# One hybrid encoder block on one core: a PSUM pool of its own for the conv taps' running sum, the relative-bias table made near the front, and the conv weights' transposes moved behind the first projection

## The chip, the cores and the metric

The kernel runs on one core of one Trainium2 chip. Its time is the device time of one execution in microseconds (us). Five engines work side by side, each through its own list of instructions in order: TensorE does matmuls (PE in the profile; PEld is its weight load), VectorE (DVE) and ScalarE (ACT) do elementwise work and read what matmuls leave in PSUM, GpSimd (POOL) does elementwise work in SBUF, and SyncE (SP) issues the DMA transfers. They meet through semaphores alone. PSUM, into which every matmul writes, is used here as eight banks of 512 float32 words for each of 128 partitions.

## The reference

One layer with 1024 tokens of width 1024, all in float32. Cut to what matters:

```python
h = rms_norm(x, norm_in_g)
proj = h @ w_in                       # split into q, k, v, z_a, q_idx, k_idx, w_idx, glu_in, z_b, gate_a, gate_b
# sparse attention: 8 index heads give scores; the 256 best keys of each query are kept
scores = einsum(relu(q_idx . k_idx), w_idx);  top_idx = top_k(scores, 256)
logits = q . k[top_idx] * 0.125 + rel_bias[t5_bucket(top_idx - q_pos)]
attn = softmax(logits) @ v[top_idx]
y_a = (attn * silu(z_a)) @ w_branch_a
u = glu_in[..., :512] * sigmoid(glu_in[..., 512:])
c = causal_depthwise_conv(u, conv_w) + conv_b          # 31 taps, 512 channels
y_b = (silu(layer_norm(c)) * silu(z_b)) @ w_branch_b
x = x + (sigmoid(gate_a) * y_a + sigmoid(gate_b) * y_b) @ w_out
x = x + sigmoid(rms_norm(x) @ w_ple_gate) * (p @ w_ple_proj)
out = rms_norm(x, final_norm_g)
```

The relative bias depends on the distance between key and query alone, so the kernel makes one table of 8 heads by 384 distances with a small matmul (`rel_bias` against a one-hot matrix), writes it to DRAM and spreads it over 128 partitions there.

## The kernel before

**Arithmetic.** Each float32 operand of a projection is split into a high part and the remainder (`w_hi`, `w_lo`, `h_h`, `h_l`), and a product is three matmuls: lines L199, L200 and L201 in `mm3`. A projection of 128 output rows by 512 tokens is 24 such matmuls into one PSUM bank. `mbank` hands the banks out in rotation from a list (`mbanks`), and ScalarE or VectorE empties a bank afterwards.

**Order in the program.** The front normalises and transposes `x` (L249 transposes, L254 and L255 the split). `glu(0)` makes the first 128 channels of `u`. Then come the index keys (72 rows), the index scores in three double banks called `wide` (L361 and L362, relu on ScalarE L366, weighted sum on VectorE L370), and `glu(1..3)`. Then VectorE runs the 31 taps of four channel groups (L299), while TensorE projects gates (`next_gate`: `z_a`, `z_b`, the branch gates; emptied by ScalarE L452). Between taps a binary search finds the 256th best score of each query: ScalarE counts signs (L419), VectorE narrows (L415, L424, L425, L437); the search ends in masks (L503 to L516, the last row L511). The four channel groups are normalised with two pairs of matmuls against a matrix of ones (L585 for the mean, L598 for the variance; `st` names the two banks they write). Then queries (L552 on ScalarE and L553 on VectorE empty their banks), keys (L564, L565) and values (L647, L648) are projected. Then attention, head by head: scores (L710, L711; the mask is added and the maximum taken by VectorE L718), transposes of probabilities (L770 to L778, emptied by L781 and L782), probabilities times values (L731), emptied by L736, L737 and L742; the projection of branch B is fed in between (L809 to L811). Branch A (L866), the output projection and the last gate end the program.

**Who sets the order.** The tile framework records the program, a scheduler orders each engine's list by priorities (`hp()` raises them) and by its own model of the machine, and inserts semaphore waits between instructions that touch the same tile. `tc.issue_after` pins an instruction behind another one. `stage()` hands out 512-word SBUF buffers in rotation.

**PSUM.** Banks 0 and 1 belong to the pool `ps` for the whole program. Banks 2 to 7 are `pi` in the front and `wide` during the index scores. After that a pool `pn` holds banks 2 to 5 and one tile `acc` of 1024 words, that is banks 6 and 7. The taps sum up in `acc`. When they are done, `acc` is used as two banks to the end of the program:

```python
psum += [pn.tile([128, 512], F32, name=f"bank{b}") for b in range(2, 6)]
acc[0] = pn.tile([128, 1024], F32, name="acc")
psum += [acc[0][:, 0:512], acc[0][:, 512:1024]]
```

From L616 on, `mbanks` runs over all eight banks, 6 and 7 one after the other. In attention the scores use banks 4, 5 and 6 (`LB`), the transposes 0 and 1 (`PTB`), the products with the values 2 and 7 (`OB`), and branch B bank 3.

**The two other places.** The 31 tap weights, the bias and the norm's weights arrive as 34 rows (`cv`, L267 to L270) and four transposes (L272, copied by L273 into `ccol`) turn them; the first use is `first_tap(0)` (L294). The relative-bias table is made at L535 to L542, after the gates: two loads, the matmul L539, the copy L540, the store into `d_tv` (L541) and its spreading into `d_tp` (L542), which `load_head` reads in attention.

Of the kernel before, what the change touches and what calls it, by code (L numbers as in the profile page):

```python
# [8 lines left out]
F32 = mybir.dt.float32  # L9
# [9 lines left out]
NH = 8  # L19
# [19 lines left out]
def hybrid_block(ctx: ExitStack, tc: tile.TileContext, x, p, norm_in_g, w_in, conv_w, conv_b,  # L39
                 conv_ln_g, conv_ln_b, w_branch_a, w_branch_b, w_out, ple_norm_g, w_ple_gate,  # L40
                 w_ple_proj, rel_bias, final_norm_g, onehot, out):
    nc = tc.nc
    def hp():
        return tc.high_priority(offset=8000)
# [23 lines left out]
    psum = [pp.tile([128, 512], F32, name=f"bank{b}") for b in range(2)]  # L68
    pn = tc.alloc_tile_pool(name="pi", bufs=1, space=bass.MemoryType.PSUM)
# [4 lines left out]
    def bank(b, n=512):  # L74
        if b < len(psum):
            return psum[b][:, 0:n]
        o = b % 2 * 512
        return wide[(b - 2) // 2][:, o:o + n]
# [15 lines left out]
    d_tv = dr.tile([NH, 384], F32, name="d_tv")  # L94
    d_tp = dr.tile([NH, 128, 384], F32, name="d_tp")
# [10 lines left out]
    def const(n):  # L106
        o = cw[0]
        cw[0] += n
        return cslab[:, o:o + n]

    ident = const(128)
# [4 lines left out]
    ccol = const(4 * 34).rearrange("p (c k) -> p c k", c=4)  # L116
# [33 lines left out]
    def stage(dt=F32):  # L150
        sn[0] += 1
        return spools[sn[0] % len(spools)]("g", dt)
# [7 lines left out]
    def load_w(src, cols, nk_=NK, g=None, pool=None, prio=True):  # L160
        if pool is None:
            wn[0] += 1
            pool = wpools[wn[0] % len(wpools)]
        w = sum(c[1] for c in cols)
        per = min(nk_, pool.tags["raw"][0] // w)
        his, los = [], []
        for a in range(0, nk_, per):
            raw = k3(pool("raw")[:, 0:per * w], per)
            hi = k3(pool("hi", F32R)[:, 0:per * w], per)
            lo = k3(pool("lo", F32R)[:, 0:per * w], per)  # L170
            o = 0
            for c0, n in cols:
                nc.sync.dma_start(raw[:, :, o:o + n], src[:, a:a + per, c0:c0 + n])
                o += n
            with hp() if prio else nullcontext():
                if g is None:
                    nc.scalar.copy(hi, raw)  # L177
                    nc.gpsimd.tensor_tensor(lo, raw, f(hi), op=OP.subtract)  # L178
                else:
                    for k in range(per):  # L180
                        gk = g[:, a + k:a + k + 1]
                        nc.scalar.activation(hi[:, k], raw[:, k], AF.Copy, scale=gk)
                        nc.vector.scalar_tensor_tensor(lo[:, k], raw[:, k], gk, f(hi[:, k]), OP.mult, OP.subtract)
            his += [hi[:, k] for k in range(per)]
            los += [lo[:, k] for k in range(per)]
        return his, los
# [16 lines left out]
    last_mm = [None]  # L203
# [3 lines left out]
    def mbank(n=512, m=128):  # L207
        b = mbanks[0][mmb[0] % len(mbanks[0])]
        mmb[0] += 1
        return bank(b, n)[0:m]  # L210

    def proj(w, c0, m, n0, n):
        o = mbank(n, m)
        mm3(o, cut(w, c0, m), hcut(n0, n))
        return o
# [14 lines left out]
    aux = bank(1)  # L230
# [10 lines left out]
    for t in range(8):  # L241
        nc.vector.tensor_scalar(xt[t], xt[t], rx[:, t:t + 1], None, OP.mult)
        if t % 4 == 3:
            c = slice((t - 3) % 4 * 128, (t % 4 + 1) * 128)
            for k in range(NK):
                b = k if t < 4 else 2 + k % 6
# [19 lines left out]
    cv = stage()  # L266
# [1 line left out]
    nc.sync.dma_start(cv[31:32], conv_b)  # L268
    nc.sync.dma_start(cv[32:33], conv_ln_g)
    nc.sync.dma_start(cv[33:34], conv_ln_b)  # L270
    for c in range(4):
        nc.tensor.transpose(aux[:, 34 * c:34 * (c + 1)], cv[0:34, 128 * c:128 * (c + 1)], ident[0:34, 0:34])  # L272
    nc.vector.tensor_copy(ccol, aux[:, 0:136].rearrange("p (c k) -> p c k", c=4))  # L273

    def glu(c, wg=None, wa=None):
        if wg is None:
            wg = load_w(win, [(C_GB + 128 * c, 128)])
            wa = load_w(win, [(C_GA + 128 * c, 128)])
        U[c] = UP("u")
        nc.gpsimd.memset(U[c][:, 0:30], 0.0)  # L280
        for hf in range(2):
            og = proj(wg, 0, 128, hf * 512, 512)
            s_ = stage()
            with hp():
                nc.scalar.activation(s_, og, AF.Sigmoid)
            oa = proj(wa, 0, 128, hf * 512, 512)
            with hp():
                nc.vector.tensor_tensor(U[c][:, 30 + hf * 512:30 + hf * 512 + 512], oa, s_, op=OP.mult)

    acc = [None]  # L290

    def first_tap(c):
        A[c] = UP("u", words=1024)
        nc.scalar.activation(A[c], U[c][:, 0:1024], AF.Identity, bias=ccol[:, c, 31:32], scale=ccol[:, c, 0:1])  # L294
# [5 lines left out]

    w_ki = load_w(win, [(C_KI, 72)])
    glu(0, w_g0, w_a0)
    first_tap(0)
    for j in range(1, EARLY + 1):
        tap(0, j)
# [28 lines left out]
    for m in range(4):  # L334
# [4 lines left out]
        for t0, n in ((256, 256), (512, 512)):  # L339
            o = proj(w, 0, 128, t0, n)  # L340
            c = slice(t0 - 256, t0 - 256 + n)
# [32 lines left out]
    pw.release()  # L374
    pn = tc.alloc_tile_pool(name="pn", bufs=1, space=bass.MemoryType.PSUM)
    psum += [pn.tile([128, 512], F32, name=f"bank{b}") for b in range(2, 6)]
    acc[0] = pn.tile([128, 1024], F32, name="acc")
    psum += [acc[0][:, 0:512], acc[0][:, 512:1024]]

    SY = Pool("sy", [("g", 512, 4)], side="right")  # L380
    spools[0:] = [SP, SY, SX, SP, SY]
# [131 lines left out]
    for ch in ENDS:  # L513
        c = slice(ch[0] - 2, ch[-1] - 1)
# [17 lines left out]
        next_gate()  # L532


    rb, oh, tv = stage(), stage(), stage()  # L535
    nc.sync.dma_start(rb[0:32, 0:8], rel_bias)
    nc.sync.dma_start(oh[0:32, 0:384], onehot)
    rbo = mbank(384)
    nc.tensor.matmul(rbo[0:8], rb[0:32, 0:8], oh[0:32, 0:384], start=True, stop=True)  # L539
    nc.vector.tensor_copy(tv[0:8, 0:384], rbo[0:8])  # L540
    nc.sync.dma_start(d_tv, tv[0:8, 0:384])  # L541
    nc.sync.dma_start(d_tp, d_tv.unsqueeze(1).to_broadcast([NH, 128, 384]))  # L542


    def queries(m):
        w = load_w(win, [(C_Q + 128 * m, 128)])
        for hf in range(2):
            t0 = hf * 512
            o = proj(w, 0, 128, t0, 512)
            a_, b_ = stage(F32R), stage(F32R)  # L550
            with hp():
                nc.scalar.activation(a_, o, AF.Copy, scale=0.125)  # L552
                nc.vector.scalar_tensor_tensor(b_, o, 0.125, f(a_), OP.mult, OP.subtract)  # L553
                for e in range(2):
                    nc.sync.dma_start(d_q[2 * m + e, 0, :, t0:t0 + 512], f(a_)[64 * e:64 * e + 64])
                    nc.sync.dma_start(d_q[2 * m + e, 1, :, t0:t0 + 512], f(b_)[64 * e:64 * e + 64])
# [10 lines left out]
                nc.sync.dma_start(d_kl[128 * m:128 * (m + 1), t0:t0 + 512], f(b_))  # L567


    st = [bank(6), bank(7)]  # L570
    z = [UP("u", words=1024) for s in range(2)]

# [401 lines left out]
    WQ.close()  # L974
    SP.close()
    CP.close()
    pn.release()
    pp.release()

# [46 lines left out]
```

## Time and profile before

| what | value |
| --- | --- |
| three runs of the kernel | 1068.12, 1069.9 and 1070.03 us, median 1069.9 us |
| the profiled execution | 1071.17 us, of which the span from the first to the last instruction is 1069.4 us |
| mean granted TensorE clock in it | 0.98 |
| instructions in the span | 13995 |

The profiled execution lies 1.3 us above the median of the runs. A row of the profile names the line of the code, the engine, the tiles as out<-in, and the time. In a list of waits the columns are the total in us, the number of waits and the longest one. In a timeline the columns are start and duration in us, and a bracket gives the idle time before the instruction and what ended it.

### The profile page before, as it was taken

How to read it: one execution, taken by the hardware profiler on the slowest of the kernel's cores; microseconds unless marked ns; L12 is line 12 of the kernel's file. 1: busy time of each engine (PE TensorE's matmuls, PEld its weight loads, DVE VectorE, ACT ScalarE, POOL GpSimd, SP SyncE). 2: the span in 40 equal slices, each digit the busy share in tenths (PEclk: the TensorE clock that was granted, in tenths of full speed). 3: DMA queues.
4: the chain of work that ended last, by engine and by line, in shares of the span. 5: the costliest groups of instructions: out<-in, count | busy, mean ns of one | idle time of the engine just before them, and what ended most of it. 6: DMA issues, size and time to landing. Idle time of an engine off the chain costs nothing.

```text
span 1069.4 us, 13995 instructions
## 1 busy us (share of the span) xinstructions
PE 1004.9 (94%) x4993; PEld 838.6 (78%) x4993; DVE 710.2 (66%) x1418; ACT 517.4 (48%) x976; POOL 282.8 (26%) x260
## 2 busy tenths in 40 slices
PE   7999999999999899994999988888799999999896
PEld 6778888888888688883889977777688778888785
DVE  5395545999999999997921177677674952242444
ACT  7444544566666788655311175555552412351422
POOL 5230202222231221352130043333423612100111
PEclk9999999999999899997999999999999999999999
DMA  7221110332232353234542375454227752020012
GB/s 246 64 60 40 40 40 21 89 116 81 89 109 80 126 162 108 60 108 97 122 149 86 97 190 145 133 153 124 89 77 262 253 215 75 5 79 1 21 59 98
DMA packets 95205, 111.45 MB, mean 104 GB/s; under 512 B 6341, under 2 KB 64765, under 8 KB 95135
## 3 DMA queue, kind: packets, MB, share of 16 engines
q1 hardware_dynamic: 95134, 110.56, 34.0%
q8 instruction: 39, 0.64, 0.2%
q14 instruction: 32, 0.25, 0.1%
HBM read 81.16 MB, written 30.95 MB: 105 GB/s over the span
## 4 chain that ended last, share of the span: by engine, by line
PE 72%; DVE 16%; ACT 4%; issue 4%; DMA 2%; POOL 1%; SPq 1%; DVEq 0%; POOLq 0%; ACTq 0%
PE bank L199 17%; PE bank L201 17%; PE bank L200 17%; DVE i_j L437 3%; PE acc L199 2%; PE acc L201 2%; PE acc L200 2%; PE acc L731 2%; DVE e_P L718 1%; PE bank L731 1%; PE bank L770 1%; PE wide L361 1%; PE wide L362 1%; DVE u_u L299 1%; DVE f_sa L869 1%
## 5 line engine op out<-in xcount | busy, mean ns | idle before, releaser
L199 PE MATMUL bank<-h_h,w_hi 128*128 128x512 f32 (+2 forms) x672 | 260.8, 389 | 1.5 <-DVE h_l L255 1.1
L201 PE MATMUL bank<-h_h,w_lo 128*128 128x512 f32 (+2 forms) x672 | 259.9, 387 | 0.0
L200 PE MATMUL bank<-h_l,w_hi 128*128 128x512 f32 (+2 forms) x672 | 259.8, 387 | 0.0
L178 POOL TENSOR_TENSOR w_lo<-w_raw,w_hi 128x1024 fp32r<-128x1024 f32 (+1 forms) x57 | 143.4, 2517 | 378.4 <-ACT w_hi L177 373.1
L419 ACT ACTIVATE i_aj<-i_S,c_d 128x384 bf16<-128x384 f32 (+3 forms) x150 | 124.4, 830 | 72.6 <-DVE c_d L415 62.3
L199 PEld LDWEIGHTS bank<-h_h,w_hi 128*128 128x128 f32 (+1 forms) x672 | 126.1, 188 | 29.7 <-issue 1.7
L200 PEld LDWEIGHTS bank<-h_l,w_hi 128*128 128x128 f32 (+1 forms) x672 | 126.3, 188 | 25.9 <-issue 0.5
L201 PEld LDWEIGHTS bank<-h_h,w_lo 128*128 128x128 f32 (+1 forms) x672 | 126.1, 188 | 26.0 <-issue 0.2
L299 DVE SCALAR_TENSOR_TENSOR acc<-u_u,c_c,acc 128x1024 f32<-128x1024 f32 x100 | 128.7, 1287 | 2.4
L177 ACT CAST w_hi<-w_raw 128x1024 fp32r<-128x1024 f32 (+1 forms) x57 | 59.2, 1039 | 82.0 <-PE acc L200 29.4
L199 PE MATMUL bank<-w_hi,g_h 128*128 128x512 f32 x224 | 87.3, 393 | 1.4 <-ACT s_g L955 1.4
L201 PE MATMUL bank<-w_hi,g_l 128*128 128x512 f32 x224 | 88.1, 395 | 0.1
L200 PE MATMUL bank<-w_lo,g_h 128*128 128x512 f32 x224 | 87.5, 391 | 0.0
L370 DVE SCALAR_TENSOR_TENSOR i_S<-wide,c_c,i_S 128x384 f32<-128x384 f32 (+5 forms) x42 | 39.2, 949 | 42.5 <-ACT wide L366 42.2
L701 POOL TENSOR_TENSOR e_mt<-m_m,ea_tp 128x256 f32<-128x256 bf16 (+1 forms) x64 | 40.7, 650 | 90.8 <-DVE c_c L718 80.0
L366 ACT ACTIVATE wide<-wide 128x384 f32<-128x384 f32 (+5 forms) x48 | 35.3, 741 | 46.8 <-PE wide L362 45.8
L721 ACT ACTIVATE e_P<-e_P,c_c 128x384 f32<-128x384 f32 (+4 forms) x64 | 49.3, 773 | 3.7 <-DVE c_c L718 3.1
L199 PEld LDWEIGHTS bank<-w_hi,g_h 128*128 128x128 f32 x224 | 42.1, 188 | 10.1 <-ACT s_g L955 1.8
L201 PEld LDWEIGHTS bank<-w_hi,g_l 128*128 128x128 f32 x224 | 42.1, 188 | 9.0 <-DVE g_l L871 0.5
L200 PEld LDWEIGHTS bank<-w_lo,g_h 128*128 128x128 f32 x224 | 42.1, 188 | 8.6
L781 ACT CAST e_pth<-bank 128x512 fp32r<-128x512 f32 x48 | 27.6, 585 | 33.7 <-PE bank L770 23.0
L437 DVE TENSOR_SCALAR_CACHE_REDUCE i_j<-i_S,c_d 128x896 bf16<-128x896 f32 (+1 forms) x36 | 43.4, 1207 | 0.0
(305 smaller groups left out, 2038.5 us busy)
## 6 DMA issues: line engine op xcount, KB each, us to landing
w_raw<-in_w_in_dram SPq DMA_DIRECT2D x48, 512.0 KB, 4.0
x_x<-in_x_dram SPq DMA_DIRECT2D x8, 512.0 KB, 4.5
s_g<-d_sb SPq DMA_DIRECT2D x16, 256.0 KB, 2.8
ea_st<-d_q SPq DMA_DIRECT2D x8, 512.0 KB, 4.0
d_yb<-s_g SPq DMA_DIRECT2D x16, 256.0 KB, 2.3
f_sa<-d_sa SPq DMA_DIRECT2D x8, 512.0 KB, 6.0
f_yb<-d_yb SPq DMA_DIRECT2D x8, 512.0 KB, 6.3
w_raw<-in_w_out_dram SPq DMA_DIRECT2D x8, 512.0 KB, 7.1
```

Of the source, the lines that this page charges most:

```text
L177: nc.scalar.copy(hi, raw)
L178: nc.gpsimd.tensor_tensor(lo, raw, f(hi), op=OP.subtract)
L199: nc.tensor.matmul(o, lh, rh, start=(k == 0), stop=False)
L200: nc.tensor.matmul(o, lh, rl, start=False, stop=False)
L201: last_mm[0] = nc.tensor.matmul(o, ll, rh, start=False, stop=(k == n - 1))
L299: return nc.vector.scalar_tensor_tensor(o_, U[c][:, j:j + 1024], ccol[:, c, j:j + 1], i_, OP.mult, OP.add)
L366: nc.scalar.activation(d, d, AF.Relu)
L370: last_score = nc.vector.scalar_tensor_tensor(s_, d, wc, s_, OP.mult, OP.add)
L419: nc.scalar.activation(ajunk[:, :nblk[i]], sblk(i), AF.Sign, bias=f(cand)[:, i - 2:i - 1], accum_out=cnt[:, i - 2:i - 1])
L437: nc.vector.tensor_scalar(junk[:, :nblk[i]], sblk(i), f(cand)[:, i - 2:i - 1], 0.0, OP.is_ge, OP.add, accum_out=cnt[:, i - 2:i - 1])
L701: nc.gpsimd.tensor_tensor(mt, MK[:, moff[i] + n - wl:moff[i] + n], tp[:, 256 - wl:256], op=OP.add)
L721: nc.scalar.activation(P, P, AF.Exp, bias=init, scale=-1.0, accum_out=sm[:, c3])
```

## The change

Three things are done.

- `acc` moves into a pool of its own, `pa`, and its halves are no longer appended to the list of banks. Just before `st` is set, `pa` is released and a second pool takes its place with two separate tiles, `bank6` and `bank7`, of 512 words each. From there on every use of banks 6 and 7 names one of these two tiles.
- The four transposes of the conv weights and their copy stand behind `glu(0)`, write bank 6 in place of bank 1, and are pinned behind the last matmul of `glu(0)`.
- The making of the relative-bias table stands behind them, with its matmul in bank 7. It no longer takes a turn in the rotation of banks and of staging buffers after the gates, but three turns of the staging rotation near the front.

```diff
-    for c in range(4):
-        nc.tensor.transpose(aux[:, 34 * c:34 * (c + 1)], cv[0:34, 128 * c:128 * (c + 1)], ident[0:34, 0:34])
-    nc.vector.tensor_copy(ccol, aux[:, 0:136].rearrange("p (c k) -> p c k", c=4))
...
     glu(0, w_g0, w_a0)
+    with tc.issue_after(last_mm[0].ins):
+        for c in range(4):
+            nc.tensor.transpose(bank(6)[:, 34 * c:34 * (c + 1)], cv[0:34, 128 * c:128 * (c + 1)], ident[0:34, 0:34])
+        nc.vector.tensor_copy(ccol, bank(6)[:, 0:136].rearrange("p (c k) -> p c k", c=4))
+
+    rb, oh, tv = stage(), stage(), stage()
+    nc.sync.dma_start(rb[0:32, 0:8], rel_bias)
+    nc.sync.dma_start(oh[0:32, 0:384], onehot)
+    rbo = bank(7, 384)
+    nc.tensor.matmul(rbo[0:8], rb[0:32, 0:8], oh[0:32, 0:384], start=True, stop=True)
+    nc.vector.tensor_copy(tv[0:8, 0:384], rbo[0:8])
+    nc.sync.dma_start(d_tv, tv[0:8, 0:384])
+    nc.sync.dma_start(d_tp, d_tv.unsqueeze(1).to_broadcast([NH, 128, 384]))
...
-    acc[0] = pn.tile([128, 1024], F32, name="acc")
-    psum += [acc[0][:, 0:512], acc[0][:, 512:1024]]
+    pa = tc.alloc_tile_pool(name="pa", bufs=1, space=bass.MemoryType.PSUM)
+    acc[0] = pa.tile([128, 1024], F32, name="acc")
...
-    rb, oh, tv = stage(), stage(), stage()
-    nc.sync.dma_start(rb[0:32, 0:8], rel_bias)
-    nc.sync.dma_start(oh[0:32, 0:384], onehot)
-    rbo = mbank(384)
-    nc.tensor.matmul(rbo[0:8], rb[0:32, 0:8], oh[0:32, 0:384], start=True, stop=True)
-    nc.vector.tensor_copy(tv[0:8, 0:384], rbo[0:8])
-    nc.sync.dma_start(d_tv, tv[0:8, 0:384])
-    nc.sync.dma_start(d_tp, d_tv.unsqueeze(1).to_broadcast([NH, 128, 384]))
...
+    pa.release()
+    pa = tc.alloc_tile_pool(name="pb", bufs=1, space=bass.MemoryType.PSUM)
+    psum += [pa.tile([128, 512], F32, name=f"bank{b}") for b in range(6, 8)]
     st = [bank(6), bank(7)]
...
+    pa.release()
     pn.release()
```

Line numbers shift by up to ten in the changed code: the transposes L272 become L301, the small matmul L539 becomes L308, the one-hot load L537 becomes L306, the statistics' matmuls L585 and L598 become L588 and L601, and lines behind them move by three. Here are three places in the order of the built programs, before and after.

TensorE, in the middle of the query projections. `h_h01` are the first 512 tokens, `h_h12` the last 512; `w3_hi56` is the second block of 128 query columns, `w_hi62` the third and `w3_hi59` the fourth. Before:

```order
L200 MATMUL acc_1182<-h_l14_112,w3_hi56_3790 128x512
L201 MATMUL acc_1182<-h_h12_110,w3_lo57_3791 128x512
L199 MATMUL bank0_58<-h_h12_110,w_hi62_3860 128x512
L200 MATMUL bank0_58<-h_l14_112,w_hi62_3860 128x512
L201 MATMUL bank0_58<-h_h12_110,w_lo63_3861 128x512
```

and 32 matmuls further on, after the 24 into bank 0 and the first eight into bank 1:

```order
L201 MATMUL bank1_59<-h_h01_109,w3_lo60_3931 128x512
L199 MATMUL bank1_59<-h_h01_109,w3_hi59_3930 128x512
L200 MATMUL bank1_59<-h_l03_111,w3_hi59_3930 128x512
L199 MATMUL acc_1182<-h_h01_109,w_hi62_3860 128x512
L200 MATMUL acc_1182<-h_l03_111,w_hi62_3860 128x512
```

After:

```order
L199 MATMUL bank6_3077<-h_h01_109,w_hi62_3869 128x512
L200 MATMUL bank6_3077<-h_l03_111,w_hi62_3869 128x512
L201 MATMUL bank6_3077<-h_h01_109,w_lo63_3870 128x512
L199 MATMUL bank7_3078<-h_h12_110,w_hi62_3869 128x512
L200 MATMUL bank7_3078<-h_l14_112,w_hi62_3869 128x512
L201 MATMUL bank7_3078<-h_h12_110,w_lo63_3870 128x512
```

Before, the projection that takes the second half of `acc` stands 32 matmuls behind the one that takes the first half; after, the two follow each other as they do in the code.

TensorE, where the small matmul stood before (`bank3` is a gate projection, `sx_g10` and `sy_g14` hold the one-hot matrix and `rel_bias`):

```order
L199 MATMUL bank3_1179<-h_h01_109,w3_hi41_3075 128x512
L200 MATMUL bank3_1179<-h_l03_111,w3_hi41_3075 128x512
L201 MATMUL bank3_1179<-h_h01_109,w3_lo42_3076 128x512
L539 MATMUL bank2_1178<-sx_g10_3062,sy_g14_3061 8x384
L199 MATMUL bank3_1179<-h_h01_109,w3_hi41_3075 128x512
```

and where it and the transposes stand after (`bank5` is the end of `glu(0)`, the rows of 72 are the index keys):

```order
L201 MATMUL bank5_66<-h_h12_110,w_lo6_205 128x512
L301 MATMUL bank6_67<-c_c1_88,sx_g1_328 128x34 x4
L201 MATMUL bank0_58<-h_h01_109,w3_lo3_335 72x512
L199 MATMUL bank1_59<-h_h12_110,w3_hi2_334 72x512
L200 MATMUL bank1_59<-h_l14_112,w3_hi2_334 72x512
L308 MATMUL bank7_68<-s_g4_449,sx_g2_448 8x384
L201 MATMUL bank1_59<-h_h12_110,w3_lo3_335 72x512
```

The small matmul has moved by some 1390 rows towards the front.

SyncE, the same stretch of the front after the change; before, the rows of `w_in` (L173) stand here alone, in the same order:

```order
L173 DMA w3_raw1_333<-in_w_in_dram 128x8x72
L305 DMA sx_g2_448<-in_rel_bias_dram 32x8
L173 DMA w_raw7_548<-in_w_in_dram 128x8x128
L173 DMA w3_raw4_683<-in_w_in_dram 128x8x128
L173 DMA w_raw10_811<-in_w_in_dram 128x8x128
L173 DMA w3_raw7_817<-in_w_in_dram 128x8x128
L306 DMA s_g4_449<-in_onehot_dram 32x384
L173 DMA w_raw13_927<-in_w_in_dram 128x8x128
L310 DMA d_tv_79<-s_g5_450 8x384
L173 DMA w_raw16_1249<-in_w_in_dram 128x8x128
L311 DMA d_tp_80<-d_tv_79 1024x1x384
L173 DMA w3_raw10_1055<-in_w_in_dram 128x8x128
```

The four transfers of the table now stand between the loads of the first weights.

## The prediction

> **What bounds the kernel now.** I read the page first: the span and the busy time of each engine.
>
> ```profile
> span 1069.4 us, 13995 instructions
> PE 1004.9 (94%) x4993; PEld 838.6 (78%) x4993; DVE 710.2 (66%) x1418; ACT 517.4 (48%) x976; POOL 282.8 (26%) x260
> ```
>
> TensorE works 94% of the span, so a gain has to come out of the 64.5 us in which it does not. Next I read what ended TensorE's idle time, in the list of waits (total us, times, longest).
>
> ```profile
> PE acc L199 <- DVE s_g L553: 14.4, 1, 14.4
> PE acc L731 <- DVE c_c L718: 9.8, 9, 2.1
> PE bank L731 <- DVE e_ao L737: 5.3, 3, 1.8
> PE bank L539 <- DMA sy_g<-in_rel_bias_dram: 4.6, 1, 4.6
> ...
> PE acc L199 <- DVE f_sa L868: 1.7, 1, 1.7
> PE bank L272 <- DMA sx_g<-in_conv_ln_b_dram: 1.6, 1, 1.6
> ...
> PE acc L199 <- DVE g_l L925: 1.4, 1, 1.4
> ```
>
> Six of these rows are touched by the change: four name `acc`, one L539, one L272. Then I looked at who else is near its limit, in stretches of the span (columns: sum, PE, PEld, DVE, ACT, POOL, granted clock, DMA).
>
> ```profile
> 180.00:345.00 165.00, 165.00 (x730) 136.60 (x729) 158.13 (x188) 100.96 (x186) 44.72 (x25) 1.00 0.30 91
> ...
> 345.00:488.00 143.00, 138.37 (x588) 111.69 (x587) 140.89 (x374) 104.68 (x207) 40.76 (x21) 0.98 0.35 108
> ...
> 531.00:600.00 69.00, 69.00 (x438) 62.88 (x437) 15.14 (x25) 14.18 (x25) 12.51 (x10) 1.00 0.43 132
> ...
> 700.00:820.00 120.00, 107.07 (x639) 91.30 (x638) 76.52 (x242) 60.47 (x135) 40.62 (x47) 0.99 0.40 122
> ```
>
> From 180 to 345 VectorE is busy 158 of 165 us and from 345 to 488 141 of 143, beside a TensorE that is as full: what TensorE gains there may meet VectorE. From 531 on VectorE is nearly free: what TensorE has won by then is kept.
>
> **Term A, the wait of 14.4 us.** The timelines of TensorE and VectorE around it:
>
> ```profile
> 478.64 0.39 PE L199 MATMUL acc<-h_h,w_hi 128*128 128x512 f32 x1
> ...
> 491.10 0.39 PE L200 MATMUL bank<-h_l,w_hi 128*128 128x512 f32 x1
> 505.86 0.80 PE L199 MATMUL acc<-h_h,w_hi 128*128 128x512 f32 x1 [14.37 <-DVE s_g L553]
> ```
>
> ```profile
> 487.56 0.68 DVE L553 SCALAR_TENSOR_TENSOR s_g<-bank,sx_g 128x512 fp32r<-128x512 f32 x1
> ...
> 505.12 0.69 DVE L553 SCALAR_TENSOR_TENSOR s_g<-acc,sx_g 128x512 fp32r<-128x512 f32 x1
> ...
> 530.73 0.68 DVE L553 SCALAR_TENSOR_TENSOR sx_g<-bank,s_g 128x512 fp32r<-128x512 f32 x1
> ```
>
> The projection that began at 478.64 filled one half of `acc`. The next one in the rotation takes the other half, and it starts when VectorE, at 505.12 + 0.69, has emptied the first. Halves alternate, so no data is shared: the wait is there because both halves are one tile. With two tiles it goes: 14.37 us. Behind it TensorE ran slowly:
>
> ```profile
> 511.15 0.44 PE L199 MATMUL acc<-h_h,w_hi 128*128 128x512 f32 x1
> ```
>
> ```profile
> 506.00:512.00 6.00, 6.00 (x16) 4.72 (x17) 5.83 (x13) 0.00 (x0) 0.00 (x0) 0.56 0.55 131
> ```
>
> The granted clock was 0.56 in these 6 us. Twelve matmuls from 505.86 to 511.15 took 5.29 us; at the full step (165.00 us for 730 from 180 to 345, 0.226) they take 2.71. That is 2.58 more, so A = 16.9 us.
>
> What is late next? A bank comes round after eight projections of 24 matmuls, 8 x 5.44 = 43.5 us. The first query projection began at 478.64 - 3 x 5.44 = 462.3; its bank is needed again at 505.8, or at 500.3 with term B, and was emptied at 487.56. The fourth is needed at 516.7 and emptied at 505.8; the eighth at 538.4 and emptied at 531.4. In the new order of VectorE the fourth to eighth L553 stand 4.0, 13.1, 7.7, 1.8 and 1.9 us of work earlier (summed over the durations before). Slack is 7 us or more everywhere, so I charge nothing; if that cover were gone, each us beyond it would come off A.
>
> **Term B, the table's wait.**
>
> ```profile
> 352.47 0.39 PE L201 MATMUL bank<-h_h,w_lo 128*128 128x512 f32 x1
> 357.49 1.33 PE L539 MATMUL bank<-sx_g,sy_g 32*8 32x384 f32 x2 [4.63 <-DMA sy_g<-in_rel_bias_dram]
> 358.75 0.80 PE L199 MATMUL bank<-h_h,w_hi 128*128 128x512 f32 x1
> ...
> 371.75 1.88 PE L585 MATMUL acc<-u_u,c_c 128*128 128x512 f32 x4
> 373.07 0.80 PE L199 MATMUL bank<-h_h,w_hi 128*128 128x512 f32 x1
> ```
>
> ```profile
> 361.96 0.54 DVE L540 COPY s_g<-bank 8x384 f32<-8x384 f32 x1
> 362.43 1.27 DVE L299 SCALAR_TENSOR_TENSOR acc<-u_u,c_c,acc 128x1024 f32<-128x1024 f32 x1
> ...
> 365.12 1.30 DVE L584 TENSOR_TENSOR u_u<-u_u,u_u 128x512 f32<-128x512 f32 x2
> ```
>
> Without it the next matmul starts at 352.70, and 45 full-speed matmuls later (10.2 us) TensorE is at the statistics at 362.9 instead of 371.75. But these need VectorE's sums L584, which end at 366.4. VectorE has no pause to make up here (141 of 143 us), so this wait takes over. In front, TensorE gets 0.33 us of transposes and 0.63 of the small matmul (half of the 1.26 us above, at full clock), say 1.0; VectorE loses L540 here (0.47) and follows TensorE's 1.0. So the second sum ends near 366.9, and the projection behind it resumes near 367.6, not at 373.07: B = 5.5 us, with a new wait of some 2.4 us inside.
>
> Would that wait slow the clock? The 2.09 us wait at 657 (below) is followed by a stretch at 0.66 over 5 us, 1.7 us lost; in the 120 us from 700 on, which hold the other two waits of 2.1 us, the clock is 0.99 on the mean, 1.2 us lost. I take none and keep 1.7 for the range. [...]
>
> **The conv transposes.** I take 0 for the 1.6 us:
>
> ```profile
> 21.29 0.41 PE L272 MATMUL bank<-c_c,sx_g 34*128 34x34 f32 x4 [1.61 <-DMA sx_g<-in_conv_ln_b_dram]
> ...
> 26.20 0.46 PE L199 MATMUL bank<-h_h,w_hi 128*72 128x512 f32 x1 [0.38 <-ACT s_g L285]
> ```
>
> ```profile
> 21.58 0.67 ACT L177 CAST w_hi<-w_raw 128x576 fp32r<-128x576 f32 x1 [1.61 <-DMA w_raw<-in_w_in_dram]
> ```
>
> TensorE next waits for ScalarE's L285, which stands behind a cast whose weights landed at 21.6 and whose transfer does not move; that wait grows by what L272's shrinks. Bound: 0 to 1.6.
>
> **Term C, attention.** TensorE, and VectorE's reads of the same two halves, at the first of three alike places; and the clock there:
>
> ```profile
> 655.01 0.34 PE L711 MATMUL acc<-ea_st,ea_st 128*128 128x384 f32 x1
> 657.44 0.39 PE L731 MATMUL acc<-e_pth,v_v 128*128 128x256 f32 x1 [2.09 <-DVE c_c L718]
> ```
>
> ```profile
> 654.05 0.42 DVE L742 TENSOR_TENSOR e_ao<-acc,e_ao 128x256 f32<-128x256 f32 x1 [0.77 <-PE acc L740]
> ...
> 656.90 0.47 DVE L718 CUSTOM_DVE_ANT_0 e_P<-acc,e_mt,c_c 128x256 f32<-128x256 f32 x1
> ```
>
> ```profile
> 657.00:662.00 5.00, 4.56 (x20) 3.98 (x21) 3.01 (x10) 1.88 (x5) 2.66 (x4) 0.66 0.28 100
> ```
>
> The product with the values (bank 7) waits for L718 to read scores from bank 6; the reader of its own bank, L742, was done at 654.5, before TensorE came at 655.35. So the three long waits, 3 x 2.09 = 6.3 us, go. The other six, 3.5 us together, are each under 1 us, and the whole order of attention is new: I leave them. Bounds: 9.8 + 1.7 (clock) = 11.5 if all goes; -3 if the new order makes waits like the 5.3 us for L737. C = 6.3.
>
> **Term D, the end.** The waits of 1.7 and 1.4 us on `acc` are of the same kind; bounds 0 to 3.1. Half, 1.5, since VectorE is the fuller engine around the first.
>
> **Sum.** 16.9 + 5.5 + 6.3 + 1.5 = 30.2. The profiled execution took 1071.2 us, which gives 1041.0; the median of the runs lies 1.3 lower, at 1069.9, which gives 1039.7. I say 1040.
>
> **Rivals.**
> 1. *VectorE takes over in the query projections.* For it: it is full up to 488. Against: the slack of 7 us, and the later evacuations move forward. If all 14.4 us come back as waits for banks (2.6 of clock too), 1069.9 - 13.3 = 1057. Chance 8%.
> 2. *Attention gives nothing.* The new order there trades one wait for another; VectorE 64%, ScalarE 50% busy speak for latency, not throughput. Half of D too: 1069.9 - 16.9 - 5.5 = 1047.5, and 1050.5 with -3. Chance 22%.
> 3. *Everything false goes.* C = 11.5, D = 3.1, the front 1.6: 1069.9 - 38.6 = 1031. Chance 15%.
> 4. *Slower: the one-hot matrix comes late.* L308 now stands at the head of TensorE's queue from about 50 us, and nothing passes it. Its load stands behind four weight loads, the last of which left at 31.52; the one behind left at 48.53.
>
> ```profile
> 31.52 0.37 SPq L173 DMA_DIRECT2D w_raw<-in_w_in_dram  x1
> ...
> 48.53 0.37 SPq L173 DMA_DIRECT2D w_raw<-in_w_in_dram  x1
> ```
>
> ```profile
> w_raw<-in_w_in_dram SPq DMA_DIRECT2D x48, 512.0 KB, 4.0
> ```
>
> A large load lands 4 us after its issue, so the matrix is there by 36. Were it held to 48.9, TensorE would wait some 3 us. Slower than before it gets when it lands after 50 + 30 = 80 us. 2%, with any other such queue. That the change does nothing would need `bank6` and `bank7` to be treated as one tile; the order shows them back to back: 1%, at 1064.
>
> **How the numbers follow.** The forecast (1035 to 1045) gets 52%, the rivals 8, 22, 15 and 3. The range of 1031 to 1055 takes in rivals 2 and 3 with their bounds and leaves out most of rival 1, the slower case and the tails. A measurement can tell about 0.2%, 2 us, from no change: faster 96%, the same 1%, slower 3%.
>
> **What would show it.** After: no wait of an L199 for L553; no wait for `rel_bias`; a wait of about 2.4 us of L588 for VectorE's sum; the last value projection some 22 us earlier; in attention no wait of the products for L718 in bank 6. The prediction is wrong if a wait for banks shows up between 490 and 540, or if the stretch of attention is as long as before.

## The result and the profile after

The changed kernel takes 1031.3 us (median of four runs, 1030.1 to 1032.0) against 1070.0 us (1068.1 to 1070.1): a ratio of 0.964, with a 95% interval of 0.962 to 0.966. The forecast was 1040 with a range of 1031 to 1055. The time lies at the lower edge of the range, at the figure of the rival in which every false wait goes; but the sum that leads there is another one, and one part of the change turned out to cost time.

The page of the changed kernel, and then what TensorE waited for in it (total us, times, longest):

```profile
span 1029.1 us, 13977 instructions
...
PE 998.2 (97%) x4993; PEld 835.3 (81%) x4993; DVE 714.7 (69%) x1418; ACT 516.5 (50%) x976; POOL 277.3 (27%) x260
```

```profile
PE bank L199 <- ACT w_hi L177: 7.5, 2, 6.7
PE bank L588 <- DVE u_u L587: 2.5, 1, 2.5
PE bank L201 <- POOL wq_lo L178: 2.2, 1, 2.2
...
PE bank L713 <- DVE c_c L721: 0.7, 1, 0.7
```

TensorE's idle time fell from 64.5 to 30.9 us, and its busy time by 6.7 us. All rows that named `acc` are gone, and so is `rel_bias`. Of the long rows two are new: L588 waits for VectorE's sum (forecast at 2.4 us, here 2.5), and a projection waits 6.7 us for its weights, which no part of the prediction had.

Where the time came from is seen best when the same work is compared. Of the 3600 projection matmuls (L199 to L201) I took the start of every hundredth in TensorE's timelines, in us; the last row is the end of VectorE's last mask (L511 before, L521 after). The columns to the right belong to experiments below.

| matmul, place | before | after | split_only | split_table | split_loads | loads_y_swap |
| --- | --- | --- | --- | --- | --- | --- |
| 1300, ahead of the statistics | 342.0 | 343.6 | 341.9 | 343.2 | 345.5 | 341.2 |
| 1400, behind the first ones | 375.3 | 372.5 | 375.0 | 370.4 | 373.0 | 370.4 |
| 1900, queries | 490.4 | 487.6 | 490.1 | 485.5 | 488.1 | 485.5 |
| 2000, keys | 530.2 | 510.3 | 512.8 | 508.2 | 510.7 | 508.2 |
| 2150, end of the keys | 564.2 | 544.3 | 546.8 | 542.2 | 544.7 | 542.2 |
| 2500, end of the values | 607.3 | 597.2 | 589.9 | 596.4 | 594.2 | 585.2 |
| 2600, branch A, behind attention | 816.4 | 780.0 | 772.9 | 779.0 | 775.6 | 774.2 |
| 3500, near the end | 1037.7 | 997.6 | 990.5 | 996.5 | 993.6 | 992.2 |
| end of the masks | 531.7 | 538.7 | 531.3 | 538.4 | 536.8 | 534.7 |

From row to row, before against after: the front loses 1.6 us, the table's place wins 4.4, the query projections win 17.1, the value projections lose 9.8, attention wins 26.3, the end wins 3.7. Together that is 40.1 us between the two profiled executions; the medians differ by 38.7. One execution can lie a few us off another at the same place: in split_y_late, whose front is that of the kernel before, the 1300th matmul starts at 343.2.

Two stretches of the changed kernel and one of the kernel before (columns as in the prediction; the second and third are attention, from the first scores to the 2600th projection matmul):

```profile
490.00:540.00 50.00, 50.00 (x223) 41.39 (x222) 41.91 (x92) 21.97 (x42) 10.08 (x8) 1.00 0.48 113
602.50:780.00 177.50, 173.21 (x1083) 149.58 (x1082) 140.36 (x467) 115.90 (x261) 73.81 (x89) 0.99 0.54 154
```

```profile
612.50:816.40 203.90, 180.33 (x1084) 154.14 (x1083) 140.79 (x465) 115.14 (x261) 73.90 (x89) 0.97 0.46 131
```

Where the 14.4 us wait stood, TensorE now works all 50 us at full clock. Attention does the same 1080 matmuls in 177.5 us in place of 203.9: 19.3 us less idle time (4.3 against 23.6) and 7.1 us less busy time, at a clock of 0.99 in place of 0.97.

The loss at the values, followed from engine to engine in the timelines of the changed kernel. TensorE, ScalarE, SyncE and VectorE:

```profile
557.82 0.80 PE L199 MATMUL bank<-w_hi,h_h 128*128 128x256 f32 x2 [6.73 <-ACT w_hi L177]
```

```profile
537.39 2.95 ACT L628 CAST y_y<-u_u 128x1024 fp32r<-128x1024 f32 x3 [14.19 <-DVE i_eq L519]
540.25 1.05 ACT L177 CAST w_hi<-w_raw 128x1024 fp32r<-128x1024 f32 x1
...
556.73 1.04 ACT L177 CAST w_hi<-w_raw 128x1024 fp32r<-128x1024 f32 x1 [2.96 <-DMA w_raw<-in_w_in_dram]
```

```profile
541.80 0.32 SPq L566 DMA_DIRECT2D d_kh<-sx_g  x1
548.90 0.32 SPq L567 DMA_DIRECT2D d_kl<-s_g  x1
...
551.36 0.60 SPq L173 DMA_DIRECT2D w_raw<-in_w_in_dram  x1
```

```profile
538.38 0.36 DVE L521 TENSOR_SCALAR m_m<-m_m 128x768 bf16<-128x768 bf16 x1
...
540.40 7.87 DVE L629 TENSOR_TENSOR y_y<-u_u,y_y 128x1024 fp32r<-128x1024 f32 x3
548.19 0.68 DVE L565 TENSOR_TENSOR s_g<-bank,sx_g 128x512 fp32r<-128x512 f32 x1
```

Read from the bottom: VectorE ends the masks at 538.7; then, but for the first key bank, it splits the conv branch's result (the last three L629 take 7.9 us) and only then empties the second key bank, at 548.2. SyncE's list stands still from 541.8 to 548.9 because the store of that key comes next, and the load of the last value weights stands behind it and four more stores, at 551.4. ScalarE, too, holds its casts of weights (L177) behind a cast (L628) that waits 14.2 us for the masks. The weights are cast at 556.7, and TensorE starts at 557.8 in place of 551.1.

### The profile page after: what moved, and what is told of

Same layout as the page of the kernel before. It is cut to its first block, busy times and chain, and to the rows that moved or that the text cites. A ratio compares the mean times of both kernels' runs of the same rounds, so it can differ in the third digit from the quotient of the medians.

```text
span 1029.1 us, 13977 instructions
## 1 busy us (share of the span) xinstructions
PE 998.2 (97%) x4993; PEld 835.3 (81%) x4993; DVE 714.7 (69%) x1418; ACT 516.5 (50%) x976; POOL 277.3 (27%) x260
## 4 chain that ended last, share of the span: by engine, by line
PE 53%; DVE 35%; ACT 4%; issue 3%; DMA 3%; SPq 1%; POOL 0%; DVEq 0%; POOLq 0%; ACTq 0%
DVE acc L295 13%; PE bank L199 13%; PE bank L201 13%; PE bank L200 12%; PE bank L734 3%; DVE i_j L447 3%; DVE c_t L435 2%; DVE c_k L434 2%; DVE u_u L295 2%; ACT i_aj L429 2%; PE bank L773 2%; PE wide L371 1%; PE wide L372 1%; DMA w_raw<-in_w_in_dram 1%; PE bank L812 1%
## 5 line engine op out<-in xcount | busy, mean ns | idle before, releaser
L199 PE MATMUL bank<-h_h,w_hi 128*128 128x512 f32 (+2 forms) x720 | 279.8, 389 | 3.2 <-ACT s_g L281 1.2
L200 PE MATMUL bank<-h_l,w_hi 128*128 128x512 f32 (+2 forms) x720 | 278.4, 387 | 0.0
L201 PE MATMUL bank<-h_h,w_lo 128*128 128x512 f32 (+2 forms) x720 | 277.8, 386 | 0.0
L199 PEld LDWEIGHTS bank<-h_h,w_hi 128*128 128x128 f32 (+1 forms) x720 | 134.9, 187 | 32.8 <-ACT s_g L281 1.6
L201 PEld LDWEIGHTS bank<-h_h,w_lo 128*128 128x128 f32 (+1 forms) x720 | 134.9, 187 | 28.1 <-issue 1.2
L199 PE MATMUL bank<-w_hi,g_h 128*128 128x512 f32 x256 | 100.2, 393 | 0.0
L200 PE MATMUL bank<-w_lo,g_h 128*128 128x512 f32 x256 | 100.0, 393 | 0.0
L201 PE MATMUL bank<-w_hi,g_l 128*128 128x512 f32 x256 | 100.0, 391 | 0.0
L177 ACT CAST w_hi<-w_raw 128x1024 fp32r<-128x1024 f32 (+1 forms) x57 | 59.0, 1038 | 73.4 <-PE bank L201 28.3
L199 PEld LDWEIGHTS bank<-w_hi,g_h 128*128 128x128 f32 x256 | 48.1, 188 | 9.8
L201 PEld LDWEIGHTS bank<-w_hi,g_l 128*128 128x128 f32 x256 | 48.1, 188 | 9.7
L724 ACT ACTIVATE e_P<-e_P,c_c 128x384 f32<-128x384 f32 (+4 forms) x64 | 49.6, 776 | 11.0 <-DVE c_c L721 10.5
L959 DVE TENSOR_TENSOR s_g<-bank,s_g 128x512 f32<-128x512 f32 (+1 forms) x17 | 11.2, 661 | 63.0 <-ACT s_g L958 63.0
L199 PE MATMUL bank<-w_hi,h_h 128*128 128x256 f32 x128 | 37.1, 293 | 6.8 <-ACT w_hi L177 6.7
```

The lines of the kernel that those rows point to most:

```text
L199: nc.tensor.matmul(o, lh, rh, start=(k == 0), stop=False)
L200: nc.tensor.matmul(o, lh, rl, start=False, stop=False)
L201: last_mm[0] = nc.tensor.matmul(o, ll, rh, start=False, stop=(k == n - 1))
L724: nc.scalar.activation(P, P, AF.Exp, bias=init, scale=-1.0, accum_out=sm[:, c3])
```

## The experiments

All ratios are to the kernel before, timed beside it on the same chip; 0.001 is about 1.07 us. The changed kernel stands at 0.964.

| run | ratio | 95% interval |
| --- | --- | --- |
| split_only | 0.956 | 0.953 to 0.958 |
| moves_only | 1.000 | 0.998 to 1.002 |
| pair_from_attention | 0.988 | 0.985 to 0.992 |
| split_from_attention | 0.972 | 0.970 to 0.975 |
| pair_roles | 0.973 | 0.971 to 0.974 |
| split_table | 0.961 | 0.960 to 0.963 |
| split_loads | 0.958 | 0.956 to 0.961 |
| y_late | 0.958 | 0.956 to 0.959 |
| split_y_late | 0.954 | 0.953 to 0.956 |
| y_late_swap | 0.962 | 0.961 to 0.964 |
| loads_y_swap | 0.959 | 0.957 to 0.961 |
| table_y_raw | 0.954 | 0.952 to 0.956 |

### The parts of the change alone

**split_only** is the kernel before with this edit and no move:

```diff
-    acc[0] = pn.tile([128, 1024], F32, name="acc")
-    psum += [acc[0][:, 0:512], acc[0][:, 512:1024]]
+    pa = tc.alloc_tile_pool(name="pa", bufs=1, space=bass.MemoryType.PSUM)
+    acc[0] = pa.tile([128, 1024], F32, name="acc")
...
+    pa.release()
+    pa = tc.alloc_tile_pool(name="pb", bufs=1, space=bass.MemoryType.PSUM)
+    psum += [pa.tile([128, 512], F32, name=f"bank{b}") for b in range(6, 8)]
     st = [bank(6), bank(7)]
```

> The kernel before with the accumulator in its own pool and two single banks behind it; the table and the conv transposes stay where they were. Theory 1 (the parts add, each worth what the prediction said): the 4.6 us wait for rel_bias and the slow clock behind it come back, 5.5 us more than the changed kernel, 1037. Rival (the wait for VectorE's sums at the statistics ends last either way, so the table's place is worth next to nothing): 1031 to 1033.

Both fell: 1023.3 us (1022.6 to 1025.2), 8 us faster than the whole change. What TensorE waits for in it, and the last load of value weights in SyncE's list:

```profile
PE bank L539 <- DMA sy_g<-in_rel_bias_dram: 4.5, 1, 4.5
PE bank L201 <- POOL wq_lo L178: 2.2, 1, 2.2
```

```profile
541.69 0.60 SPq L173 DMA_DIRECT2D w_raw<-in_w_in_dram  x1
```

The table's wait is there, and still the kernel is faster than the changed one: its masks end at 531.3 (538.7 in the changed kernel), the weights are asked for at 541.7 (551.4), and TensorE has no wait at the values. The table above shows the trade: the changed kernel is 2.5 us ahead from the statistics to the keys and 7.3 us behind after the values.

**moves_only** is the changed kernel with the old `acc` to the end.

> The changed kernel with the 1024-word accumulator kept as banks 6 and 7 to the end; the table and the transposes stand near the front. Theory 1: 1070.0 - 5.5 = 1064.5, and the 14.4 us wait of the query projections is back. Rival (moves worth nothing, or the front 1.4 us longer as the changed trace shows): 1068 to 1071.

The rival held: a ratio of 1.000. TensorE's waits:

```profile
PE acc L199 <- DVE sx_g L553: 15.2, 1, 15.2
PE acc L731 <- DVE c_c L718: 9.8, 9, 2.1
```

What TensorE wins at the table (372.5 in place of 375.3 at the 1400th matmul) is gone by the queries: the false wait there is set by VectorE and is 0.8 us longer, and L598 waits 2.9 us. VectorE's masks end at 536.8 here (531.7 before), though TensorE comes to the keys no earlier.

### The two places of the split

**pair_from_attention** takes one tile for banks 6 and 7 from attention on:

```diff
+    pa.release()
+    pa = tc.alloc_tile_pool(name="pc", bufs=1, space=bass.MemoryType.PSUM)
+    pair = pa.tile([128, 1024], F32, name="pair")
+    psum[6:8] = [pair[:, 0:512], pair[:, 512:1024]]
     spools[0:] = [SP]
     SX.close()
```

> The changed kernel, but from attention on banks 6 and 7 are again one tile of 1024 words; TensorE's list up to attention is the same row for row. By the prediction's terms (C 6.3, D 1.5): 1031.3 + 7.8 = 1039. By the two traces (idle time of TensorE in attention 23.6 against 4.3 us, half-clock stretches there 13.7 against 3.4 us, end 5.6 against 2.2 us): 19.3 + 5.1 + 3.4 = 27.8, so 1059. Rival (attention gained because the projections before it end earlier, or by the table's earlier load, not by its own banks): 1031 to 1034.

1058.3 us, as the two traces had it: 27.0 us more than the changed kernel, where the prediction's terms C and D give 7.8. TensorE's list up to attention is the same as in the changed kernel, row for row, so all of it lies in attention and behind. Its waits and its stretch of attention:

```profile
PE pair L738 <- DVE c_c L725: 9.4, 9, 2.1
...
PE bank L738 <- DVE e_ao L744: 5.3, 3, 1.8
PE bank L777 <- DVE e_ptl L789: 2.6, 2, 2.1
```

```profile
602.90:806.60 203.70, 180.13 (x1081) 153.70 (x1081) 141.38 (x466) 115.15 (x261) 73.95 (x89) 0.97 0.47 131
```

The stretch is as long as before the change (203.9). The false waits themselves are 9.4 us of it. The other rows are true dependencies (bank 2, the probabilities), and they go too when the pair is split: without the false edges the scheduler writes another order, in which 4.3 us of idle time are left in all.

**split_from_attention** keeps the old `acc` until the values are projected.

> The changed kernel, but banks 6 and 7 stay one tile of 1024 words until the values are projected, and are two tiles in attention and behind it. By the prediction's term A (16.9 us all kept): 1031.3 + 16.9 = 1048. By the two traces (the wait of 14.4 us and 2.6 of clock went, but 7.2 us of new waits and about 2.1 us of clock came in the value projections): 1031.3 + 7.7 = 1039. Attention as long as in the changed kernel, 178 us from the first scores to the last product, in both.

1041.7 us. The second working (1039) came nearer than the first (1048): at the 2000th matmul this kernel is 20.3 us behind the changed one (530.6 against 510.3), at the 2500th 10.5 (607.7 against 597.2), since it has no wait at the values. TensorE's longest wait is the old one, and attention takes 183.3 us from the 2500th to the 2600th projection matmul, as in the changed kernel (182.8):

```profile
PE acc L199 <- DVE sx_g L554: 15.2, 1, 15.2
```

**pair_roles** asks which coupling costs attention its time.

```diff
-    LB, PTB, OB = [4, 5, 6], [0, 1], [2, 7]
+    LB, PTB, OB = [4, 5, 3], [0, 1], [2, 7]
-    mbanks[0] = [3]
+    mbanks[0] = [6]
```

> pair_from_attention (1058.3) with the scores in banks 4, 5 and 3 and branch B in bank 6, so that the pair 6 and 7 couples branch B with every second product and no longer the scores with it. Theory F (attention's 27 us are the coupling of scores and products: TensorE's product waits for VectorE to read scores of the other half, and the scheduler orders all of attention around it): most of it goes, 1031 to 1040. Rival (any two banks in one tile cost attention this much, since each is written by one stage while the other is read): 1050 to 1060.

1043.5 us, between the two. Attention:

```profile
601.40:788.20 186.80, 177.72 (x1081) 149.12 (x1080) 146.19 (x465) 116.72 (x263) 74.81 (x90) 0.99 0.49 136
```

Of the 26.2 us that the pair costs attention (203.7 less 177.5), 16.9 are the coupling of scores and products; some 9 stay with a pair that couples branch B and every second product (the new roles without a pair were not run). The 3.8 us behind attention stay as well (matmuls 2600 to 3500: 221.4 us here and with the pair, 217.6 in the changed kernel).

### What the moved table costs

**split_table** is split_only with the table moved as in the changed kernel, the transposes left.

> split_only with the table made near the front as in the changed kernel; the conv transposes stay in their old place. The changed kernel is 8 us slower than split_only: TensorE wins 4.3 us at the table's old place, loses 1.8 in the front and 9.9 at the value projections, whose weights come late. Theory V (the search and the masks on VectorE set when these weights are cast, so TensorE's gain ahead of them is lost, and whatever makes VectorE later is added): 1023 at best, 1031 if the table's place alone makes VectorE as late as in the changed kernel. Rival (the moved transposes did the harm, by the slow clock in the front): 1023.3 - 4.3 = 1019.

0.961, some 6 us slower than split_only: theory V's second case. The rival fell; with the table moved alone the masks end at 538.4, and the waits at the values are back (5.7 and 2.1 us). The time shows that the table's place costs these 6 us. How it makes the masks late is not shown: in split_y_late below, where the table stands in its old place, they end at 536.7. The transposes' share would be what is left to 0.964; the two intervals touch, so it can't be told from nothing.

**split_loads** moves the table's two loads alone; its matmul stays, so TensorE's list is that of split_only.

```diff
+    ro = CP("o")
+    rb, oh = ro, ro[:, 8:392]
+    nc.sync.dma_start(rb[0:32, 0:8], rel_bias)
+    nc.sync.dma_start(oh[0:32, 0:384], onehot)
...
-    rb, oh, tv = stage(), stage(), stage()
-    nc.sync.dma_start(rb[0:32, 0:8], rel_bias)
-    nc.sync.dma_start(oh[0:32, 0:384], onehot)
+    tv = stage()
```

> split_only (0.9556 of the kernel before) with the two loads of the table alone moved near the front, into a buffer of their own; its matmul stays in its old place, and TensorE's list is otherwise the same. The 4.6 us wait for rel_bias goes. Theory T (VectorE's search and masks end later because TensorE is at the statistics earlier, and the value weights with them): the masks end at 536 or later in place of 531.3, the wait at the value projections appears, and the time is no better than 0.9556, up to 0.962. Rival (the table's matmul and copy in the front make VectorE late): the masks stay at 531 and the 4.3 us are kept: 0.9515, 1018 to 1019.

0.958, no better than split_only (the intervals overlap), though the 4.5 us wait is gone. The masks end at 536.8, the value weights are waited for 4.9 us. So theory T's outcome came, but not cleanly: in the profiled execution 3.6 us of the 5.5 us by which the masks are late are there at the 1300th matmul already, behind two stretches at half clock (from 15.6 and 83.9) that split_only's execution does not have.

**y_late** takes the split of the conv branch's result out of the way, on the changed kernel:

```diff
     for c in range(4):
-        nc.scalar.copy(Yh[c], A[c])
-        nc.vector.tensor_tensor(Yl[c], A[c], f(Yh[c]), op=OP.subtract)
+        with tc.issue_after(last_k[0].ins):
+            nc.scalar.copy(Yh[c], A[c])
+        with tc.issue_after(last_k[1].ins):
+            nc.vector.tensor_tensor(Yl[c], A[c], f(Yh[c]), op=OP.subtract)
```

(the block stands behind the keys, and `last_k` holds the last key's evacuations).

> The changed kernel; the split of the conv branch's result into Yh and Yl, which waits for the memory that the masks leave, stands behind the last key's evacuation on ScalarE and on VectorE and no longer ahead of the casts of the value weights and of the keys' evacuations. Theory V (the weights' casts and the SyncE list stood behind that split): the waits of 7.2 us and the slow clock behind them go, 9.9 us: 1021.4. Rival (the load of the weights itself is late, held by its buffer or by the busy DMA queues): 1029 to 1031. Worse if branch B then waits for Yl: above 1031.

0.958: by the ratios some 7 us less than the changed kernel, and in the profiled executions 5.6 us less at the 2500th matmul (591.6 against 597.2), of the 9.8 us lost there. Its masks end even later (541.1). What is left of the wait, 2.3 us at 554, ends with a weight load that still stands behind stores:

```profile
548.17 0.38 SPq L173 DMA_DIRECT2D w_raw<-in_w_in_dram  x1
```

**split_y_late**

> The same edit on split_only, where TensorE has no wait at the value projections: 1023.3, no change, by theory V (its weights were cast 0.2 us before TensorE came). If y_late comes out below this run, the two moves of the change are worth something once VectorE's end no longer sets the values: 2 us by the two traces (4.3 - 1.8).

0.954, no change against split_only, as expected. It is not as clean as that: in this execution the masks end at 536.7, 5.4 us later than in split_only, and TensorE still has no wait at the values. y_late did not come out below it.

**y_late_swap** and **loads_y_swap** change the two pools of the value weights over (`pool=(WP, WX)[c]`), so that the first half's weights are loaded before 525 us.

> y_late (0.9575 of the kernel before) with the two buffers of the value weights changed over: the first half's weights now come through the pool whose loads SyncE issues before 525, not through the one whose last load stood behind the keys' stores (issued at 548.2, cast at 552.9). If that load is what is left of the wait: the 3.6 us of waits at 548 and 554 go, 0.954. If VectorE's late masks hold the values in another way: as y_late, 0.9575.

> split_loads with both edits of y_late_swap. If VectorE's lateness reaches TensorE by the value weights alone, TensorE keeps the 4.3 us of the table's wait here: 0.9556 - 0.004 = 0.9515, and the fastest of all. If masks and keys' evacuations hold it through the banks or through the first scores: 0.955 to 0.958.

Both hopes fell: 0.962, which is slower than y_late, and 0.959. Both kernels have a new wait at the first scores of attention, 5.9 and 6.0 us. In the second, the waits at the values are gone and TensorE is 4.7 us ahead of split_only at the 2500th matmul (585.2 against 589.9). Then this, TensorE and SyncE:

```profile
596.67 1.09 PE L720 MATMUL bank<-ea_st,ea_st 128*128 128x128 f32 x3 [6.00 <-DMA ea_st<-d_kh]
```

```profile
590.62 0.32 SPq L692 DMA_DIRECT2D ea_st<-d_q  x1
```

The first loads of attention were asked for at 590.6 (572.2 in split_only). That fits the memory of `ea`, the pool of attention's operands: it lies where the weights' second pool was, which now frees last. This was read from the lists and not tried by itself.

**table_y_raw** is split_table with y_late's edit and, in place of the swap, a second raw buffer: `WX = Pool("w3", [("raw", 1024, 2), ...`.

> split_table (0.9613 of the kernel before) with the split into Yh and Yl behind the keys as in y_late, and a second raw buffer in the pool of the first half of the value weights, so that their last load stands ahead of the keys' stores in SyncE's list; the value weights keep their pools, and the first loads of attention their memory. TensorE is 4.6 us ahead of split_only from the statistics to the value projections (split_table: 485.5 against 490.1). If VectorE's lateness reaches TensorE by these weights alone, this is kept: 0.9556 - 0.0043 = 0.951, the fastest of all. If each way that is opened shows the next one (as the swap of the buffers showed the first loads of attention): 0.954 to 0.958.

0.954 (1022.3 us), the second case by its interval's middle: split_only, split_y_late and this one can't be told apart. The wait at the values is down to 1.1 us and the first loads of attention are in time, but the masks of this execution end at 544.4, and TensorE had been 3.1 us late at the 1300th matmul. None of the kernels kept the table's 4.3 us to its end.

## Why the prediction was right, and where it was not

**Term A (16.9) was right**: 17.1 us between matmuls 1900 and 2000, and no wait for a bank from 490 to 540. The check of what is late next was right for the banks it looked at, and looked at nothing else. **The step that failed is the sentence that VectorE is nearly free from 531 on, so that what TensorE has won by then is kept.** It read VectorE's load in the kernel before. The search and the masks are one chain on VectorE; in the changed kernel they end 7 us later, TensorE arrives 20 us earlier, and behind the masks stand the casts and loads of the value weights. The cover of those weights was TensorE's own wait of 14.4 us. The last value projection, forecast some 22 us earlier, comes 10 us earlier (597.2 against 607.3). This cost 9.8 us, of which y_late gets more than half back; rival 1 had the engine right and the place and the carrier wrong: weights through ScalarE's and SyncE's lists at the values, not banks at the queries. Why the masks end later stays open: they do so in every kernel with the moves, but in split_y_late without them too.

**Term B (5.5) had its mechanism and lost its worth.** The new wait is where it was forecast:

```profile
367.12 3.41 PE L588 MATMUL bank<-u_u,c_c 128*128 128x512 f32 x4 [2.48 <-DVE u_u L587]
369.54 1.42 PE L199 MATMUL bank<-h_h,w_hi 128*128 128x512 f32 x1
```

```profile
367.00:372.00 5.00, 4.88 (x10) 2.69 (x11) 4.52 (x22) 3.33 (x9) 0.00 (x0) 0.66 0.51 153
```

But the clock fell behind it (0.66 over 5 us; I had kept these 1.7 us for the range), and the front lost 1.6 us in place of 1.0, so the net at the 1400th matmul is 2.8. And split_only shows that the move is a loss at the end: 8 us in the changed kernel with both moves, some 6 with the table's alone.

**The conv transposes (0)** went as argued in one point: TensorE still waits for ScalarE's L285 (now L281), until 26.17 in place of 26.20. What the argument left out is the clock:

```profile
26.17 0.70 PE L199 MATMUL bank<-h_h,w_hi 128*72 128x512 f32 x1 [1.18 <-ACT s_g L281]
```

```profile
26.00:31.00 5.00, 4.83 (x14) 2.82 (x15) 1.49 (x1) 1.16 (x2) 3.18 (x2) 0.66 0.59 162
```

A half-clock stretch follows (0.50 from 26.20 to 29.61). split_from_attention has the same list for TensorE in the front and no such stretch, and is 1.3 us earlier at the 1300th matmul (342.3 against 343.6). Of the seven profiled executions with this list four have the stretch (343.6 to 344.0) and three have not (342.2 to 342.3), so most of the front's 1.6 us is the chance of one execution and not the price of the change.

**Term C (6.3) was the mis-sized one**: 26.3 us. The bound of 11.5 counted the waits that name `acc`, and one stretch of slow clock. pair_from_attention shows that the false edges cost 26.2 us there, of which only 9.4 stand under their own name; the rest is true waits of another order, and clock. That I left the whole order of attention at its old waits was the step. How much of the 26 is order and how much the direct wait was not separated further, since no run could hold the order and take the edges away. **Term D (1.5)** is 3.7, above its bound of 3.1.

So 30.2 became 40.1 by two errors of opposite sign: 20 and 2 us too little in C and D, 10 and 3 too much in what follows A and in B. That the time still lies in the range, and only just, is luck: some 22 us too little were set against some 13 too much. Rival 3's 1031 is met, but not by its mechanism.

## What to carry to other kernels

Two buffers that are halves of one tile can cost more than the waits that carry the tile's name: a scheduler orders everything around the false edge, and the true waits of that order bear other names. So bound such a term by the idle time of the whole stretch and its slow clock (here 23.6 us, and some 6 us by a clock of 0.97 over 203.9 us; 26.3 were won), not by the rows that name it. When a long wait goes, ask of every engine, not of the banks alone, what the waiting engine will meet next, and follow the queues of loads and casts that stand behind a late engine. And time the parts of a change apart: here one part alone (0.956) beats the whole (0.964), and the other part alone is worth nothing (1.000).

## What the runs showed of the hardware

**Seventeen VectorE instructions beside a GpSimd instruction took 0.8 to 2.3 us longer than the shortest of their kind.** One more, and the GpSimd instruction beside it, in the changed kernel:

```profile
510.86 0.16 DVE L532 TENSOR_TENSOR c_t<-c_c 128x3 f32<-128x3 f32 x1
511.06 2.26 DVE L533 TENSOR_SCALAR c_c<-c_t 128x3 f32<-128x3 f32 x1
513.35 0.16 DVE L534 TENSOR_TENSOR c_t<-c_t,c_c 128x3 f32<-128x3 f32 x1
```

```profile
510.87 2.42 POOL L178 TENSOR_TENSOR w_lo<-w_raw,w_hi 128x1024 fp32r<-128x1024 f32 x1
```

Three elements for each partition take 2.26 us, between two rows of three elements that take 0.16, and end at 513.3 with the GpSimd instruction. From 345 to 540, 17 VectorE instructions are more than 0.8 us longer than the shortest of their kind, 28.4 us together, and all 17 lie beside a GpSimd instruction (split_only, up to the end of its masks: 16 and 23.3); 15 of the 17 end within 0.03 us of its end. The one shown is the only one of its shape and is not counted. These longer durations are part of why the masks end 7.4 us later than in split_only: from the program's start to there VectorE is idle 2.5 us more, and about 5 us are longer durations of the same instructions. No run isolated it, and no trace shows its cause.

**Behind waits of 1.2 to 2.5 us TensorE's clock was 0.66 over 5 us in some places and 1.00 in others.** In the changed kernel it was 0.66 behind 2.48 us at 367 and behind 1.18 us at 26; it did not fall at 26 in split_from_attention, with the same list and a wait of 1.17 us. In the kernel before, it was 0.66 from 657 to 662, at the first of three alike waits of 2.09 us, and 1.00 at the other two, which end at 707.1 and 755.1:

```profile
705.00:710.00 5.00, 2.91 (x21) 2.64 (x21) 3.89 (x15) 2.50 (x6) 3.10 (x4) 1.00 0.15 52
753.00:758.00 5.00, 2.91 (x21) 2.63 (x21) 3.87 (x15) 2.50 (x6) 3.08 (x4) 1.00 0.17 52
```

A clock of 0.66 over 5 us is 1.7 us lost. So such a wait cost 1.7 us more in one place and nothing in another, and two executions of the same list differ by it, here by 1.3 us at the 1300th matmul. What decides it was not shown.
